# Moving the tiles that TensorE reads to multiples of 256 bytes by padding small tiles, in a two-layer decoder trunk

## The chip, the cores and the metric

One core of a Trainium2 chip. The metric is the device time of one launch, in microseconds. Before the change three runs gave 1027.2, 1028.49 and 1031.6 us; their median, 1028.49 us, is the time before.

## The reference

The kernel computes two decoder layers on x of 512 tokens by 1024. Layer 0 mixes by a gated DeltaNet, layer 1 by a gated short convolution; both have a norm ahead and one behind.

```python
for i in range(DEPTH):                                    # DEPTH = 2
    h = rms_norm(x, pre_norm_w[i])
    y = gated_deltanet_mixer(h, ...) if i == 0 else short_conv_mixer(h, ...)
    x = x + rms_norm(y, post_norm_w[i])

def gated_deltanet_mixer(h, w_in, conv_w, a_log, dt_bias, norm_w, w_out):
    qkv, z, b_logit, a_logit = split(h @ w_in)            # 1024 x 6176
    q, k, v = split(silu(causal_depthwise_conv(qkv, conv_w)))
    q, k = l2_normalize(q), l2_normalize(k)               # 8 heads of 128, each for two of v's 16
    o = chunked_gated_delta_rule(q, k, v, g, beta)        # a triangular solve and a scan over chunks
    return (rms_norm(o, norm_w) * silu(z)) @ w_out        # 2048 x 1024

def short_conv_mixer(h, w_in, conv_w, w_out):
    u, b, c, z = split(h @ w_in)                          # 1024 x 8192
    return (b * causal_depthwise_conv(c * u, conv_w) * silu(z)) @ w_out   # 2048 x 1024
```

All of it is float32.

## The kernel before, in words

**Products.** Each large product is taken in float32r as a sum of three: both operands are split into a high part and a rest, and `mm3` (lines 183 to 186) issues high x high, rest x high and high x rest into one PSUM bank:

```python
nc.tensor.matmul(ps, lhsT=lh, rhs=rh, start=start, stop=False)
nc.tensor.matmul(ps, lhsT=lh, rhs=rl, start=False, stop=False)
nc.tensor.matmul(ps, lhsT=ll, rhs=rh, start=False, stop=stop)
```

`lhsT` is the stationary operand (128 columns of 4 bytes, 512 bytes of a partition), `rhs` the moving one (512 columns, 2048 bytes; 256 columns, 1024 bytes, in a few units of layer 1). Which tiles these are depends on the place:
- `unit` (line 188), the input projections of both layers, into tiles pp: stationary are 128 columns of a weight (tiles whi and wlo, or the two halves of w3), moving are the activations hh and hl (at the very start xh and xl). `weights` (line 171) loads a weight into a raw tile, then ACT or POOL writes the high part and DVE the rest; every third weight goes to w3, so that three are in work.
- `out_products`, the output projection of layer 0, into pa: stationary are the gated outputs of the heads (hh and hl again for heads 0 to 7, oh2 and ol2 for 8 to 11, oh3 and ol3 for 12 to 15), moving are the weights.
- `product`, the output projection of layer 1, into pf: stationary yh and yl, moving whi and wlo (for the last three of 16 steps hh and hl, which then hold weights).

The profile prints names without their numbers: w3 shows as w, oh2 and oh3 as oh, ol2 and ol3 as ol.

**Order.** PE's instructions stand in the order in which the code issues them; chains of smaller work (the norms, the solve, the scan, the gates) are emitted between the steps of products by the class `Pump`, from planned times and a table of corrections. The other engines are ordered by a scheduler. The weights come by the queue of SP.

**Addresses.** Each pool is one stretch of a partition's memory, and its tags follow each other in it: the constants, the weights (wp), the gate values (gt, which ends with par), hh and hl (hp), then es, sm and dl. es holds, after twelve large buffers, two buffers of the tag tm (lines 642 to 646: DVE writes a product to it and subtracts it at once); sm holds small columns, odd among them (line 622, read once by DVE); dl holds ktok, E, zT, nv, S, qg, kT, d2, Vr, then nrm (line 566, written by POOL, read by ACT as a scale) and, behind it, qT, junk and d3. A tile's start is rounded up to 32 bytes and to no more, so a small tile's size sets where all that follow begin. yh, yl and the second w3 lie where dl was.

Of the kernel before, what the change touches and what calls it, by code (L numbers as in the profile page):

```python
# [10 lines left out]
F32 = mybir.dt.float32  # L11
# [7 lines left out]
P = 128  # L19
# [6 lines left out]
NC = T // P  # L26
# [84 lines left out]
def trunk_kernel(ctx, tc, xT, x, cols, rows, eye, post0, pre1, post1, w_in, w_out, sw_in, sw_out, out):  # L111
# [6 lines left out]
    sw_in_v = sw_in.rearrange("(k p) n -> p k n", p=P)  # L118
    sw_out_v = sw_out.rearrange("(k p) n -> p k n", p=P)
    xT_v = xT.rearrange("(k p) t -> p k t", p=P)  # L120

    cst = ctx.enter_context(tc.tile_pool(name="cst", bufs=1))
    dram = ctx.enter_context(tc.tile_pool(name="dram", bufs=1, space=DRAM))
# [37 lines left out]
    def pd(shape, name):  # L161
        return ps_d.tile(shape, F32, tag="pd", name=name)
# [37 lines left out]
    def rsqrt(pool, y, shape, tag, vector=False):  # L200

        r = pool.tile(shape, F32, tag=tag + "r", name=tag + "r")
        t = pool.tile(shape, F32, tag=tag + "t", name=tag + "t")
        nc.vector.tensor_scalar(out=r.bitcast(I32), in0=y.bitcast(I32), scalar1=-0.5, scalar2=float(0x5f3759df),
                                op0=ALU.mult, op1=ALU.add)
        for _ in range(3):
            if vector:
                nc.vector.tensor_tensor(out=t, in0=r, in1=r, op=ALU.mult)
                nc.vector.scalar_tensor_tensor(out=t, in0=t, scalar=-0.5, in1=y, op0=ALU.mult, op1=ALU.mult)
                nc.vector.scalar_tensor_tensor(out=r, in0=t, scalar=1.5, in1=r, op0=ALU.add, op1=ALU.mult)  # L210
            else:
                nc.gpsimd.tensor_tensor(out=t, in0=r, in1=r, op=ALU.mult)
                nc.gpsimd.tensor_tensor(out=t, in0=t, in1=y, op=ALU.mult)
                nc.gpsimd.tensor_scalar(out=t, in0=t, scalar1=-0.5, scalar2=1.5, op0=ALU.mult, op1=ALU.add)
                nc.gpsimd.tensor_tensor(out=r, in0=r, in1=t, op=ALU.mult)
        return r
# [8 lines left out]
    gt = ctx.enter_context(tc.tile_pool(name="gt", bufs=1))  # L225
    hp = ctx.enter_context(tc.tile_pool(name="hp", bufs=1))
    es = ctx.enter_context(tc.tile_pool(name="es", bufs=2))
    sm = ctx.enter_context(tc.tile_pool(name="sm", bufs=2))
# [19 lines left out]
    with ExitStack() as L0:  # L248
        dl = L0.enter_context(tc.tile_pool(name="dl", bufs=2))
# [104 lines left out]
        y, m, t, u, r = (sm.tile([P, NH, NC], F32, tag="gs" + n, name="gs" + n, bufs=1) for n in "ymtur")  # L354
# [140 lines left out]
        def c_kq(gs, kh, w, ps, tl):  # L495
            while not gates_done and kh:
                yield 0.1
            silu = conv_silu(ps, (QK // P if w == 0 else 0) + 2 * gs.g + kh, tl)
            while not gates_done:
                yield 0.1  # L500
            while before_silu:
                before_silu.pop()()
            while gs.g == 0 and (kh or w) and not normed_k:
                yield 0.1
            silu()
            (gs.qT if w else gs.kT)[kh] = tl
            pump.add((c_qnorm if w else c_est)(gs, kh))
            yield 0
# [30 lines left out]
        def norms(tl, ss):  # L539

            junk = dl.tile([P, P], F32, tag="junk", name="junk", bufs=1)
            tok = pd([P, NC, P], "tok")
            for c in range(NC):
                nc.tensor.transpose(out=tok[:, c], in_=tl[:, c * P:(c + 1) * P], identity=ident)
            pump.pe(0.43, False)
            for c in range(NC):
                last_sq = nc.scalar.activation(junk, tok[:, c], AF.Square, accum_out=ss[:, c:c + 1])
            nc.vector.tensor_scalar_add(ss, ss, EPS)
            return tok, last_sq
# [10 lines left out]
        def c_est(gs, kh):  # L560
            g = gs.g
            while not gates_done or (g > 1 and not groups[g - 2].done):
                yield 1
            kT = gs.kT[kh]
            if kh == 0:
                gs.nrm = dl.tile([P, 2, NC], F32, tag="nrm", name="nrm")
                gs.epsa = dl.tile([P, 2, NC], F32, tag="epsa", name="epsa")
                gs.bp, gs.bpe = (dl.tile([P, 4, NC], F32, tag=n, name=n) for n in ("bp", "bpe"))
                gs.E = dl.tile([P, 16, P], F32, tag="E", name="E", bufs=2)
            yield (11 if g else 4,)  # L570
            ss = sm.tile([P, NC], F32, tag="ssn", name="ssn")
            tok, last_sq = norms(kT, ss)
            ktok = dl.tile([P, NC, P], F32, tag="ktok", name="ktok", bufs=4)
            kte = 0 if g == 0 else 1
            if kte == 1:
                nc.scalar.copy(ktok, tok)
            gs.ktok[kh] = ktok
            normed_k.append(1)
            kk = pd([P, NC, P], "kk")
            for c in range(NC):  # L580
                s = slice(c * P, (c + 1) * P)
                nc.tensor.matmul(kk[:, c], lhsT=kT[:, s], rhs=kT[:, s], start=True, stop=True)
            pump.pe(0.9, False)
            rk2 = sm.tile([P, 1, NC], F32, tag="rk2", name="rk2")
            nc.vector.reciprocal(rk2[:, 0], ss)
            h2, g2 = slice(2 * kh, 2 * kh + 2), slice(4 * g + 2 * kh, 4 * g + 2 * kh + 2)
            nc.vector.tensor_tensor(out=gs.bp[:, h2], in0=beta[:, g2], in1=rk2.to_broadcast([P, 2, NC]), op=ALU.mult)
            for r in range(2):
                hl_, h = 2 * kh + r, 4 * g + 2 * kh + r
                if g == 0:  # L590
                    dt = dt0[h]
                else:
                    dt = es.tile([P, NC, P], F32, tag="dt", name="dt")
                    nc.sync.dma_start(out=dt, in_=dt_d[h])
                for c in range(NC):
                    nc.scalar.activation(dt[:, c], dt[:, c], AF.Copy, scale=gs.bp[:, hl_, c:c + 1])
                last_e = nc.vector.tensor_tensor(out=gs.E[:, 4 * hl_:4 * hl_ + 4], in0=kk, in1=dt, op=ALU.mult)
                nc.sync.dma_start(out=dt_d[h], in_=dt)
            if kte == 0:
                nc.vector.tensor_copy(ktok, tok)  # L600
            if g == 0:
                fence[:] = last_e, last_sq
            nc.vector.tensor_tensor(out=gs.bpe[:, h2], in0=gs.bp[:, h2], in1=edec[:, g2], op=ALU.mult)
            rk = rsqrt(sm, ss, [P, NC], "rk")
            nc.gpsimd.tensor_tensor(out=gs.nrm[:, kh], in0=ss, in1=rk, op=ALU.mult)  # L605
            gs.est += 1
            if gs.est == 2:
                pump.add(c_solve(gs))

        def c_solve(gs):  # L610
# [7 lines left out]
            E = gs.E  # L618
            blk = lambda i, n=32: slice(n * i, n * i + n)
            if not parity:  # L620
                odd = sm.tile([P, 1], F32, tag="odd", name="odd", bufs=1)
                nc.vector.tensor_reduce(out=odd, in_=ident.rearrange("p (a c k) -> p c a k", c=2, k=16)[:, 1],
                                        op=ALU.add, axis=mybir.AxisListType.XY)
                par = gt.tile([P, 16, 2], F32, name="par")
                nc.vector.tensor_copy(par[:, :, 1:2], odd[:, :, None].to_broadcast([P, 16, 1]))
                nc.vector.tensor_scalar(out=par[:, :, 0:1], in0=par[:, :, 1:2], scalar1=-1.0, scalar2=1.0,
                                        op0=ALU.mult, op1=ALU.add)
                parity.append(par)
# [10 lines left out]
            for i in range(31, 0, -1):  # L639
                m0 = i // 2  # L640
                w = 16 - m0
                t = es.tile([P, 136], F32, tag="tm", name="tm")
                tv = t[:, :i * w].rearrange("p (m j) -> p m j", j=i)
                nc.vector.tensor_tensor(out=tv, in0=N[:, i:i + 1, 0:i].to_broadcast([P, w, i]),
                                        in1=X[:, m0:, i:i + 1].to_broadcast([P, w, i]), op=ALU.mult)
                nc.vector.tensor_tensor(out=X[:, m0:, 0:i], in0=X[:, m0:, 0:i], in1=tv, op=ALU.subtract)  # L646
# [541 lines left out]
```

## Time and profile before

| | us |
|---|---|
| median of three runs | 1028.49 (1027.2 to 1031.6) |
| the profiled execution | 1028.76 |
| its span, first to last instruction | 1026.6 |
| PE busy | 974.4 (95%) |
| DVE busy | 612.3 (60%) |
| ACT busy | 420.6 (41%) |
| POOL busy | 235.4 (23%) |
| mean granted clock of TensorE | 0.978 of 2.4 GHz |

The layers follow each other in time: layer 0 takes until about 570 us, the input projections of layer 1 until about 930 us, and the last product with the last norm the rest. A product's duration in the trace covers its way through the array, so neighbours overlap: what a product costs in a row of products is the distance between two starts. The addresses of operands aren't in the trace; they come from the program that was built.

### The profile page before, as it was taken

Reading aid. Unit: us, or ns where it says so; the run is one execution under the profiler, and the core shown is the slowest. Engines: PE = TensorE matmul, PEld = TensorE weight load, DVE = VectorE, ACT = ScalarE, POOL = GpSimd, SP = SyncE. Lnnn points to the kernel's source line nnn. Section 1 sums busy time; section 2 is a strip of 40 time slices with the busy share of each in tenths; the row PEclk is TensorE's granted clock in tenths of the full one; section 3 lists DMA queues with packets and bytes.
Section 4 is the critical chain, followed back from the end, with each engine's and each line's share of the span. In section 5 each row is a group of like instructions: output and inputs, shape, how many; then the busy total and the mean of one; then the engine's idle time right before and its main releaser. Section 6 shows DMA issues by size and latency. Waiting matters only on the chain.

```text
span 1026.6 us, 14732 instructions
## 1 busy us (share of the span) xinstructions
PE 974.4 (95%) x5430; PEld 805.7 (78%) x5430; DVE 612.3 (60%) x1100; ACT 420.6 (41%) x1002; POOL 235.4 (23%) x446
## 2 busy tenths in 40 slices
PE   7957999989999999999998999999999999999997
PEld 5845778877788788888776899888888888888885
DVE  8678998746986784734469976433433433333133
ACT  4575764526545553334212554232222322322123
POOL 6264631344135223335633000000000000000001
PEclk9987999999999999999999999999999999999999
DMA  6334673255235622793645556333233332323322
GB/s 193 89 109 124 211 240 84 63 156 162 76 100 151 178 63 82 218 330 128 197 145 182 163 169 188 110 91 103 83 101 93 92 103 84 102 82 102 103 83 82
DMA packets 172391, 133.91 MB, mean 130 GB/s; under 512 B 6272, under 2 KB 146176, under 8 KB 171936
## 3 DMA queue, kind: packets, MB, share of 16 engines
q1 hardware_dynamic: 172176, 132.88, 43.1%
q8 instruction: 43, 0.70, 0.3%
q14 instruction: 28, 0.23, 0.1%
q10 hardware_dynamic: 144, 0.09, 0.0%
HBM read 117.16 MB, written 15.79 MB: 130 GB/s over the span
## 4 chain that ended last, share of the span: by engine, by line
PE 75%; DVE 9%; DMA 6%; ACT 4%; issue 3%; POOL 2%; SPq 0%; POOLq 0%; DVEq 0%; ACTq 0%
PE pp L184 17%; PE pp L186 17%; PE pp L185 17%; PE pf L185 3%; PE pf L184 2%; PE pf L186 2%; PE pa L186 2%; PE pa L185 2%; PE pa L184 2%; PE u L758 2%; DVE wlo L167 1%; DMA gb<-gt_d 1%; PE po L792 1%; PE psn L772 1%; PE p L748 1%
## 5 line engine op out<-in xcount | busy, mean ns | idle before, releaser
L184 PE MATMUL pp<-hh,whi 128*128 128x512 f32 (+1 forms) x624 | 239.2, 383 | 5.1 <-DVE acc L470 2.1
L185 PE MATMUL pp<-hl,whi 128*128 128x512 f32 (+1 forms) x624 | 233.3, 374 | 1.0 <-DVE r L987 1.0
L186 PE MATMUL pp<-hh,wlo 128*128 128x512 f32 (+1 forms) x624 | 233.3, 374 | 0.0
L167 DVE TENSOR_TENSOR wlo<-wraw,whi 128x1024 fp32r<-128x1024 f32 x115 | 141.4, 1229 | 135.5 <-ACT whi L166 110.1
L166 ACT CAST whi<-wraw 128x1024 fp32r<-128x1024 f32 x64 | 67.2, 1050 | 189.8 <-PE pp L185 112.2
L184 PEld LDWEIGHTS pp<-hh,whi 128*128 128x128 f32 x624 | 119.1, 191 | 26.8 <-POOL nrm L605 2.5
L186 PEld LDWEIGHTS pp<-hh,wlo 128*128 128x128 f32 x624 | 118.8, 190 | 22.2
L185 PEld LDWEIGHTS pp<-hl,whi 128*128 128x128 f32 x624 | 119.1, 191 | 21.1 <-DVE hl L167 1.2
L184 PE MATMUL pp<-hh,w 128*128 128x512 f32 (+1 forms) x304 | 116.1, 382 | 0.0
L186 PE MATMUL pp<-hh,w 128*128 128x512 f32 (+1 forms) x304 | 113.2, 373 | 1.1 <-DVE w L167 1.1
L185 PE MATMUL pp<-hl,w 128*128 128x512 f32 (+1 forms) x304 | 113.2, 372 | 0.0
L1144 POOL TENSOR_TENSOR ob<-ob,ytNa 128x384 f32<-128x384 f32 x2 | 2.1, 1040 | 458.0 <-ACT ob L1143 458.0
L166 POOL CAST whi<-wraw 128x1024 fp32r<-128x1024 f32 x51 | 62.1, 1219 | 94.0 <-PE pp L185 60.8
L167 DVE TENSOR_TENSOR w<-wraw,w 128x1024 fp32r<-128x1024 f32 x50 | 62.6, 1252 | 33.8 <-ACT w L166 31.7
L186 PEld LDWEIGHTS pp<-hh,w 128*128 128x128 f32 x304 | 57.3, 189 | 12.4 <-DVE w L167 1.5
L184 PEld LDWEIGHTS pp<-hh,w 128*128 128x128 f32 x304 | 57.5, 189 | 10.3 <-issue 0.4
L185 PEld LDWEIGHTS pp<-hl,w 128*128 128x128 f32 x304 | 57.3, 189 | 9.7
L470 DVE SCALAR_TENSOR_TENSOR acc<-pp,col,acc 128x511 f32<-128x511 f32 (+2 forms) x72 | 53.6, 745 | 14.4 <-ACT acc L467 13.5
L166 ACT CAST w<-wraw 128x1024 fp32r<-128x1024 f32 x25 | 26.2, 1047 | 67.8 <-PE pp L185 48.6
L185 PE MATMUL pf<-wlo,yh 128*128 128x512 f32 x104 | 41.5, 399 | 0.0
L184 PE MATMUL pf<-whi,yh 128*128 128x512 f32 x104 | 41.0, 394 | 0.0
L646 DVE TENSOR_TENSOR Na<-Na,tm 128x126 f32<-128x126 f32 (+22 forms) x124 | 39.4, 317 | 2.7
(310 smaller groups left out, 1724.8 us busy)
## 6 DMA issues: line engine op xcount, KB each, us to landing
wraw<-in_sw_in_dram SPq DMA_DIRECT2D x76, 512.0 KB, 4.0
wraw<-in_w_in_dram SPq DMA_DIRECT2D x47, 512.0 KB, 4.0
wraw<-in_w_out_dram SPq DMA_DIRECT2D x32, 512.0 KB, 4.1
wraw<-in_sw_out_dram SPq DMA_DIRECT2D x16, 512.0 KB, 3.5
eg<-gt_d SPq DMA_DIRECT2D x16, 256.0 KB, 4.2
dtq<-dt_d SPq DMA_DIRECT2D x16, 256.0 KB, 3.9
gb<-gt_d SPq DMA_DIRECT2D x3, 1024.0 KB, 6.6
dt_d<-gb SPq DMA_DIRECT2D x3, 1024.0 KB, 4.9
```

Of the source, the lines that this page charges most:

```text
L166: (nc.scalar.copy if hi_eng is None else hi_eng.tensor_copy)(dst_hi, src)
L167: nc.vector.tensor_tensor(out=dst_lo, in0=src, in1=dst_hi.bitcast(F32), op=ALU.subtract)
L184: nc.tensor.matmul(ps, lhsT=lh, rhs=rh, start=start, stop=False)
L185: nc.tensor.matmul(ps, lhsT=lh, rhs=rl, start=False, stop=False)
L186: nc.tensor.matmul(ps, lhsT=ll, rhs=rh, start=False, stop=stop)
L470: nc.vector.scalar_tensor_tensor(out=acc[:, s:], in0=ps[:, :T - s], scalar=w(j), in1=acc[:, s:], op0=ALU.mult, op1=ALU.add)
L646: nc.vector.tensor_tensor(out=X[:, m0:, 0:i], in0=X[:, m0:, 0:i], in1=tv, op=ALU.subtract)
L748: nc.tensor.matmul(p1[:, 2 * kh:2 * kh + 2], lhsT=gs.kT[kh][:, s], rhs=S[:, 2 * kh:2 * kh + 2], start=True, stop=True)
L758: nc.tensor.matmul(u[:, a], lhsT=gs.E[:, 4 * a + c], rhs=X[:, a] if c else gs.nv[a][:, c], start=True, stop=True)
L772: nc.tensor.matmul(psn[:, 2 * kh:2 * kh + 2], lhsT=gs.ktok[kh][:, c], rhs=Vk[:, 2 * kh:2 * kh + 2], start=True, stop=True)
L792: nc.tensor.matmul(po[:, a], lhsT=gs.qkd[a][:, c], rhs=Vr[:, a], start=c == 0, stop=True)
L1144: nc.gpsimd.tensor_tensor(out=ob[:, m], in0=ob[:, m], in1=yt[c][:, m], op=ALU.add)
```

## The change

Four small tiles are allocated larger than what is used of them: par twice as large (128 bytes more), tm 768 bytes for 544, odd 64 for 4, nrm 96 for 32. The names then stand for the part that was there before. (An empty line at the top of the function moves all later line numbers by one.)

```diff
--- before.py
+++ after.py
@@ -118,6 +118,7 @@
     sw_in_v = sw_in.rearrange("(k p) n -> p k n", p=P)
     sw_out_v = sw_out.rearrange("(k p) n -> p k n", p=P)
     xT_v = xT.rearrange("(k p) t -> p k t", p=P)
+
 
     cst = ctx.enter_context(tc.tile_pool(name="cst", bufs=1))
     dram = ctx.enter_context(tc.tile_pool(name="dram", bufs=1, space=DRAM))
@@ -563,7 +564,7 @@
                 yield 1
             kT = gs.kT[kh]
             if kh == 0:
-                gs.nrm = dl.tile([P, 2, NC], F32, tag="nrm", name="nrm")
+                gs.nrm = dl.tile([P, 6, NC], F32, tag="nrm", name="nrm")[:, :2]
                 gs.epsa = dl.tile([P, 2, NC], F32, tag="epsa", name="epsa")
                 gs.bp, gs.bpe = (dl.tile([P, 4, NC], F32, tag=n, name=n) for n in ("bp", "bpe"))
                 gs.E = dl.tile([P, 16, P], F32, tag="E", name="E", bufs=2)
@@ -618,10 +619,10 @@
             E = gs.E
             blk = lambda i, n=32: slice(n * i, n * i + n)
             if not parity:
-                odd = sm.tile([P, 1], F32, tag="odd", name="odd", bufs=1)
+                odd = sm.tile([P, 16], F32, tag="odd", name="odd", bufs=1)[:, 0:1]
                 nc.vector.tensor_reduce(out=odd, in_=ident.rearrange("p (a c k) -> p c a k", c=2, k=16)[:, 1],
                                         op=ALU.add, axis=mybir.AxisListType.XY)
-                par = gt.tile([P, 16, 2], F32, name="par")
+                par = gt.tile([P, 2, 16, 2], F32, name="par")[:, 0]
                 nc.vector.tensor_copy(par[:, :, 1:2], odd[:, :, None].to_broadcast([P, 16, 1]))
                 nc.vector.tensor_scalar(out=par[:, :, 0:1], in0=par[:, :, 1:2], scalar1=-1.0, scalar2=1.0,
                                         op0=ALU.mult, op1=ALU.add)
@@ -639,7 +640,7 @@
             for i in range(31, 0, -1):
                 m0 = i // 2
                 w = 16 - m0
-                t = es.tile([P, 136], F32, tag="tm", name="tm")
+                t = es.tile([P, 192], F32, tag="tm", name="tm")
                 tv = t[:, :i * w].rearrange("p (m j) -> p m j", j=i)
                 nc.vector.tensor_tensor(out=tv, in0=N[:, i:i + 1, 0:i].to_broadcast([P, w, i]),
                                         in1=X[:, m0:, i:i + 1].to_broadcast([P, w, i]), op=ALU.mult)
```

No engine's list of instructions differs, in operations, shapes, order or waits. What differs is where tiles lie. The offset of a tile's start from the last multiple of 256 bytes:

| tiles | before | after |
|---|---|---|
| whi, wlo, the raw weights | 0 | 0 |
| hh, hl | 128 | 0 |
| acc, vT, dt, qkd (es, ahead of tm) | 128 | 0 |
| tm, its two buffers | 128, 160 | 0, 0 |
| X, eg (es, behind tm) | 192 | 0 |
| ktok, E and oh3, zT and ol3, w3, nv, S, qg, kT and oh2, d2, Vr | 160 | 0 |
| yh, yl (layer 1) | 160 | 0 |
| qT and ol2, junk, d3 (behind nrm) | 32 | 0 |
| ident, ones, utri, ltri (constants) | 128 | 128 |
| g of the gates, rx | 64, 224 | 128, 32 |
| ac and zs, ob (layer 1, for DVE, ACT and DMA alone) | 0, 192 | 96, 32 |

By pairs of operands (moving/stationary), the products of `mm3` are, before: 1518 at 128/0, 120 at 0/128 and 2 at 128/128; 796 at 128/160, 420 at 0/160, 24 at 0/32, 150 at 160/0, 82 at 160/128, 72 at 160/160 and 8 at 160/32; those of 256 columns 384 at 128/0 and 192 at 128/160. After: 3180 at 0/0, 12 at 0/128, and 576 of 256 columns at 0/0.

## Rows read from the trace of the kernel before

**Rows 1.** The page: busy time by engine, and PE and DVE by slices.

```profile
PE 974.4 (95%) x5430; PEld 805.7 (78%) x5430; DVE 612.3 (60%) x1100; ACT 420.6 (41%) x1002; POOL 235.4 (23%) x446
...
PE   7957999989999999999998999999999999999997
...
DVE  8678998746986784734469976433433433333133
```

**Rows 2.** The page: chain that ended last, by engine and by line.

```profile
PE 75%; DVE 9%; DMA 6%; ACT 4%; issue 3%; POOL 2%; SPq 0%; POOLq 0%; DVEq 0%; ACTq 0%
PE pp L184 17%; PE pp L186 17%; PE pp L185 17%; PE pf L185 3%; PE pf L184 2%; PE pf L186 2%; PE pa L186 2%; PE pa L185 2%; PE pa L184 2%; PE u L758 2%; DVE wlo L167 1%; DMA gb<-gt_d 1%; PE po L792 1%; PE psn L772 1%; PE p L748 1%
```

**Rows 3.** Busy time of the engines by stretch (columns in its second line).

```profile
core 0: us, PE busy (x) PEld busy (x) DVE busy (x) ACT busy (x) POOL busy (x), PEclk, DMA share, GB/s
0.00:100.00 100.00, 75.01 (x348) 58.67 (x349) 75.83 (x135) 58.71 (x132) 47.55 (x62) 0.88 0.42 127
...
200.00:300.00 100.00, 93.72 (x643) 78.91 (x642) 70.33 (x161) 49.89 (x167) 38.00 (x94) 0.97 0.42 121
...
600.00:700.00 100.00, 100.00 (x599) 88.49 (x598) 51.23 (x65) 37.66 (x56) 0.00 (x0) 1.00 0.46 133
...
900.00:1000.00 100.00, 100.00 (x431) 80.60 (x430) 29.93 (x30) 23.21 (x25) 0.00 (x0) 1.00 0.32 95
...
544.70:547.30 2.60, 2.60 (x8) 1.99 (x7) 2.53 (x6) 0.86 (x4) 2.60 (x1) 0.51 0.85 269
```

**Rows 4.** Timeline of PE, hh against whi: start, duration, instruction.

```profile
852.85 0.40 PE L184 MATMUL pp<-hh,whi 128*128 128x512 f32 x1
853.09 0.40 PE L185 MATMUL pp<-hl,whi 128*128 128x512 f32 x1
...
862.61 0.40 PE L184 MATMUL pp<-hh,whi 128*128 128x512 f32 x1
```

**Rows 5.** Timeline of PE, hh against w3 (printed w).

```profile
847.02 0.40 PE L186 MATMUL pp<-hh,w 128*128 128x512 f32 x1
...
851.92 0.39 PE L186 MATMUL pp<-hh,w 128*128 128x512 f32 x1
```

**Rows 6.** Timeline of PE, the last product.

```profile
949.22 0.39 PE L184 MATMUL pf<-whi,yh 128*128 128x512 f32 x1
949.45 0.40 PE L185 MATMUL pf<-wlo,yh 128*128 128x512 f32 x1
949.69 0.39 PE L186 MATMUL pf<-whi,yl 128*128 128x512 f32 x1
...
956.22 0.39 PE L184 MATMUL pf<-whi,yh 128*128 128x512 f32 x1
```

**Rows 7.** Timeline of PE at half clock.

```profile
544.74 0.62 PE L184 MATMUL pa<-whi,oh 128*128 128x512 f32 x1
...
547.29 0.63 PE L184 MATMUL pa<-w,oh 128*128 128x512 f32 x1
```

**Rows 8.** Timeline of PE, w3 against oh3 and ol3, behind that stretch.

```profile
548.84 0.39 PE L186 MATMUL pa<-w,ol 128*128 128x512 f32 x1
549.07 0.39 PE L184 MATMUL pa<-w,oh 128*128 128x512 f32 x1
...
550.20 0.39 PE L186 MATMUL pa<-w,ol 128*128 128x512 f32 x1
```

**Rows 9.** Timeline of PE, w3 against oh3 and ol3, two other places.

```profile
515.31 0.40 PE L184 MATMUL pa<-w,oh 128*128 128x512 f32 x1
...
516.71 0.49 PE L184 MATMUL pa<-w,oh 128*128 128x512 f32 x1
...
557.91 0.40 PE L184 MATMUL pa<-w,oh 128*128 128x512 f32 x1
...
560.71 0.40 PE L184 MATMUL pa<-whi,oh 128*128 128x512 f32 x1
```

**Rows 10.** Timeline of PE, products of 256 columns.

```profile
581.32 0.28 PE L184 MATMUL pp<-hh,w 128*128 128x256 f32 x1
...
583.80 0.28 PE L184 MATMUL pp<-hh,w 128*128 128x256 f32 x1
...
584.87 0.28 PE L184 MATMUL pp<-hh,whi 128*128 128x256 f32 x1
...
589.73 0.28 PE L186 MATMUL pp<-hh,wlo 128*128 128x256 f32 x1
```

**Rows 11.** Chain in order of time: start, us, what.

```profile
129.01 5.80 DMA dt_d<-gb
...
332.92 7.48 DMA og_d<-ohs
```

**Rows 12.** DMA issues: size each, median us to landing.

```profile
dt_d<-dt SPq DMA_DIRECT2D x12, 256.0 KB, 3.3
og_d<-ohs SPq DMA_DIRECT2D x12, 256.0 KB, 2.6
...
dt_d<-gb SPq DMA_DIRECT2D x4, 256.0 KB, 2.1
```

## The prediction

> **What bounds the kernel now.** I read the page first. PE is busy 95% of the span, and in the 40 slices its digit is 9 from about 100 us to the end almost without a break, while DVE has 60% and ACT 41% [rows 1]. The chain that ended last says the same in another way: 75% of it is PE, and the nine PE entries for the destinations pp, pf and pa at lines 184 to 186 add up to 64% (17+17+17, 3+2+2, 2+2+2) [rows 2]. These are the products of `mm3`, so 0.64 x 1026.6 = 657 us of the path consist of one kind of instruction. The table by stage shows no other engine near PE from 600 us on (PE 100 of 100 us, DVE 51 to 30) [rows 3]. DMA has 6% of the chain [rows 2].
>
> Then I read the timeline for the distance from the start of one product to the next. The busy figure of one product (0.39 to 0.40 us) says nothing on the rate, since products overlap. With 512 columns at 2.4 GHz the columns alone are 512/2.4 = 213.3 ns. The trace has more: 42 products from 852.85 to 862.61 us, 232.4 ns each [rows 4]; 21 from 847.02 to 851.92 us, 233.3 ns [rows 5]; 30 from 949.22 to 956.22 us, 233.3 ns [rows 6]. At the granted clock of 0.5 six products take 2.55 us, 425 ns each, which is 512/1.2 = 427 and nothing more [rows 3, 7]. So at the upper level some 19 ns of 233 are not columns, and at the lower level they are absent. These 19 ns, 657 x 19/233 = 54 us of the path, are all that addresses could win in the products.
>
> **The change part by part.** No instruction is added, removed or moved: each engine has the same list in the same order with the same waits. Four tiles get larger, and by that every tile allocated behind them starts elsewhere. Of `mm3`'s 3768 products, 3192 have 512 columns and 576 have 256. Before, no pair has both operands at a multiple of 256 bytes; after, all but 12 of the 3768 have (the address table stands with the change). The four padded tiles themselves are used by DVE and POOL in the same shapes, so nothing is charged for them.
>
> Addresses of each sort can be compared inside this one trace, as the buffers differ:
> - moving operand at 128 (hh, hl), stationary at 0 (whi, wlo): 232.4 ns [rows 4]
> - moving at 128, stationary at 160 (the third buffer w3, printed as w): 233.3 ns [rows 5]
> - moving at 0 (whi, wlo), stationary at 160 (yh, yl): 233.3 ns [rows 6]
> - both at 160 (w3 with the last four heads, oh3 and ol3): six products from 548.84 to 550.20 us, 226.7 ns each [rows 8]; with operands of the same offsets six from 515.31 to 516.71 us, 233.3 ns, and twelve from 557.91 to 560.71 us, 233.3 ns [rows 9].
> So putting one operand at a multiple of 256 buys at most 0.9 ns (0.4%), whichever operand it is. What both at 0 do is not in the trace. Two rows are near to it. By the distance from a boundary it is the pair 128/0, for 0 and 128 are the two offsets that are multiples of 128: 232.4 ns. By equal offset of the two operands it is the pair 160/160: (6 x 226.7 + 18 x 233.3)/24 = 231.7.
>
> The path now: 1640 of the 3192 wide products have their operands at 0 and 128 (232.4), 1552 have one at 160 or 32 (233.3), mean 232.8. On the path 657 us / 232.8 ns = 2820 wide products, so 1 ns is worth 2.8 us. With the first near row the change gives 232.8 - 232.4 = 0.4 ns, or 1.1 us; with the second 1.1 ns, or 3.1 us. I take the second, since equal offsets are what the change makes of every pair: 3.1 us. The 256-column products bear on this little: from 584.87 to 589.73 us 41 of them take 118.5 ns each at 128/0, and from 581.32 to 583.80 us 21 take 118.1 ns at 128/160 [rows 10], so there the worse offset is even faster by 0.4 ns; 576 x 0.4 = 0.2 us, left out.
>
> The bounds: the best a product can get is 213.3 ns, 19.5 less than now, 55 us; the best run seen, 226.7, gives 6.1 x 2.8 = 17 us. The other way, the slowest spacing that comes regularly is 238 ns, the step behind L185 in the last product (949.45 to 949.69 us is 0.24) [rows 6]; if every product had it the cost would be 5.2 x 2.8 = 15 us.
>
> Other engines and DMA: DVE, ACT and POOL are off the path in the long stages, and whichever of their tiles move start at a multiple of 32 bytes before and after. The Trainium skill, SBUF — State Buffer, section Specifications (TRN2), gives lines of 16 bytes for reads of SBUF; a multiple of 32 starts such a line before and after, so by that rule the whole change is worth nothing and the time stays at 1028.8; the spread from 226.7 to 233.3 at one pair of addresses shows that start addresses are at least not the only thing that sets the spacing.
>
> DMAs out of tiles that move: dt_d<-gb 5.80 us and og_d<-ohs 7.48 us are the longest of them on the chain [rows 11]; the trace has none of this size from a 256-byte offset to compare, so I bound them by nothing and by the whole difference between the stores of 256 KB, 2.1 us (dt_d<-gb) to 3.3 us (dt_d<-dt) [rows 12], 1.2 us each and 2.4 for both, either way, and take nothing. The Trainium skill, DMA: Bandwidth & Descriptors, section How a descriptor splits into AXI transactions, says that a transfer that doesn't start on 256 bytes fetches from the boundary below; a 2048-byte row would then fetch 9 blocks where 8 do, and 13.3 us on the chain would lose an estimated ninth, 1.5 us. No run here shows it yet.
>
> Sum against the profiled execution: 1028.76 us with a span of 1026.6, 2.2 us around it; 1028.76 - 3.1 = 1025.7. The median of the three timed runs, 1028.49, lies 0.3 below the profiled one; I keep 1025.7.
>
> **The rivals.**
> 1. Both operands on a boundary lock every product at the short spacing of 226.7 ns: 17 us, 1012. For it: six in a row at 226 to 227 ns, and the only stretch with equal offsets has it. Against: 18 products with the same offsets at 233.3, and the 226.7 begins right behind a stretch of half clock, which may have set its phase.
> 2. The 19 ns come from crossing boundaries and vanish: 216 ns, 16.8 x 2.8 = 47 us, 982. Against: a stationary operand at 0 and a moving operand at 0, each with another partner, leave 232.4 and 233.3. The Trainium skill, TensorE: Matmul & The Clock Gate, section Back-to-back issue gap, has N/2.4 + 2.5 ns, 216 for 512 columns; the trace disagrees in every run of wide products at 2.4 GHz that I looked at, so this page is what speaks for it.
> 3. Slower: both operands now start on the same place of a 256-byte block in every product, and the two reads meet each time. Place: all of `mm3`. Price: up to the 238 ns spacing, 15 us, 1043; it decides from 1.8 ns on (5.1 / 2.8), a mean spacing over 234.6. For it: an offset that is off by 32 beats one at a boundary in the 256-column products. Against: the stretches with equal offsets at 160 are not above 233.3.
> 4. The claim holds for `mm3` only: ident, ones, utri and ltri stay at 128, and the transposes and small products that read them can't gain. This leaves the sum as it is; nothing of it was counted.
> A shift of a microsecond or two in when PE waits can also add or remove one of the short stretches at half clock (the mean clock is 0.88 in the first 100 us and 0.97 from 200 to 300 [rows 3]); it is noise of 2 us to the forecast.
>
> **How the numbers follow.** A difference under 0.5% (5.1 us) can't be told from no change in this kernel. Chances: forecast (spacing 231 to 234.5, from 5 us faster to 5 us slower) 0.50; rival 1 and spacings between 227 and 231 0.32; rival 2 0.06; rival 3 0.12. So faster 0.38, same 0.50, slower 0.12. The likeliest case alone is 1022 to 1032. The range for 8 in 10 reaches down to rival 1, less 2 us of noise, 1010, and up to 1034, where a part of rival 3 is still inside; outside stay rival 2 and the worse half of rival 3.
>
> **What will show it.** In the profile after, the spacing of the wide products at full clock is the whole test: for hh/whi (232.4 before), for hh/w3 and for pf (233.3 before). About 231.7 in all three bears the forecast out; 226.7 is rival 1, 216 rival 2, over 234.6 rival 3. The order of the chain's entries should stay as it is. The prediction is wrong if the spacing stays at 232 to 233 and the time moves by more than 5 us: then a wait or a transfer did it, which this sum has at nothing.

## The result, and the profile after

The change made the kernel faster: 1016.27 us, median of 6 runs (1014.69 to 1019.41), against 1027.92 us for the kernel before beside it (6 runs, 1026.97 to 1031.60). The ratio is 0.988, interval 0.986 to 0.991. That is 11.7 us, more than the 5.1 us that can be told from no change. The profiled execution took 1017.51 us with a span of 1015.6, which is 11.0 us below the span before.

From the page of the kernel after (lines 185 to 187 are the three products of `mm3`, one line further down than before), busy time by engine and the chain that ended last, to lay beside [rows 1, 2]:

```profile
PE 960.8 (95%) x5430; PEld 805.5 (79%) x5430; DVE 611.7 (60%) x1100; ACT 420.1 (41%) x1002; POOL 239.6 (24%) x446
...
PE 70%; DVE 13%; DMA 7%; ACT 4%; issue 3%; POOL 3%; SPq 0%; POOLq 0%; DVEq 0%; ACTq 0%
PE pp L185 16%; PE pp L187 16%; PE pp L186 16%; PE pf L185 2%; PE pf L187 2%; PE pf L186 2%; DVE tm L645 2%; DVE wlo L168 2%; DMA eg<-gt_d 2%; DVE Na L647 2%; PE pa L186 1%; PE pa L187 1%; DMA gb<-gt_d 1%; PE pa L185 1%; PE u L759 1%
```

The counts of instructions are the same as before on every engine, and so are the busy times of DVE and ACT to within 0.6 us. Only PE is shorter, by 13.6 us; POOL has 4.2 us more, which the kernel all_128 below, with the same spacing of products, doesn't have (235.6 us). On the chain PE falls from 75% to 70%, and DVE rises from 9% to 13%: the solve (tm, line 645, and Na, line 647) is now among the fifteen dearest entries, where it was not. That this follows from the shorter products isn't shown: all_128 has 74% PE and 10% DVE and neither entry, so the chain of one execution can go either way there.

The table by stage of the kernel after (first line: columns), for [rows 3]:

```profile
core 0: us, PE busy (x) PEld busy (x) DVE busy (x) ACT busy (x) POOL busy (x), PEclk, DMA share, GB/s
0.00:100.00 100.00, 74.03 (x337) 58.57 (x338) 72.83 (x126) 57.16 (x128) 46.66 (x61) 0.85 0.41 127
...
900.00:1000.00 100.00, 100.00 (x443) 82.81 (x442) 29.52 (x32) 25.75 (x32) 0.00 (x0) 1.00 0.27 85
```

From 900 to 1000 us PE is busy throughout, at a granted clock of 1.00 in both kernels, and does 443 products where it did 431. The first 100 us go the other way: 337 instructions in place of 348, at a clock of 0.85 in place of 0.88.

The test that the prediction named is the spacing. The timeline of PE in the kernel after (start, duration, instruction), hh against whi, for [rows 4]:

```profile
846.39 0.39 PE L185 MATMUL pp<-hh,whi 128*128 128x512 f32 x1
846.62 0.39 PE L186 MATMUL pp<-hl,whi 128*128 128x512 f32 x1
...
855.91 0.39 PE L185 MATMUL pp<-hh,whi 128*128 128x512 f32 x1
```

These are 42 products in 9.52 us: 226.7 ns, where 232.4 stood. The same view, hh against w3 for [rows 5] and the last product for [rows 6]:

```profile
840.27 0.39 PE L185 MATMUL pp<-hh,w 128*128 128x512 f32 x1
...
845.03 0.39 PE L185 MATMUL pp<-hh,w 128*128 128x512 f32 x1
...
934.11 0.39 PE L185 MATMUL pf<-whi,yh 128*128 128x512 f32 x1
...
940.91 0.39 PE L185 MATMUL pf<-whi,yh 128*128 128x512 f32 x1
```

21 products in 4.76 us and 30 in 6.80 us, 226.7 ns both, where 233.3 stood. All three sorts have the spacing that the prediction gave to rival 1. The products of 256 columns, for [rows 10], went the other way:

```profile
582.50 0.28 PE L185 MATMUL pp<-hh,whi 128*128 128x256 f32 x1
...
586.47 0.28 PE L185 MATMUL pp<-hh,whi 128*128 128x256 f32 x1
```

33 products in 3.97 us, 120.3 ns, where 118.5 and 118.1 stood.

### The profile page after: what moved, and what is told of

It is laid out like the page before. It is cut to its first block, busy times and chain, and to the rows that moved or that the text cites. A ratio compares the mean times of both kernels' runs of the same rounds, so it can differ in the third digit from the quotient of the medians.

```text
span 1015.6 us, 14732 instructions
## 1 busy us (share of the span) xinstructions
PE 960.8 (95%) x5430; PEld 805.5 (79%) x5430; DVE 611.7 (60%) x1100; ACT 420.1 (41%) x1002; POOL 239.6 (24%) x446
## 4 chain that ended last, share of the span: by engine, by line
PE 70%; DVE 13%; DMA 7%; ACT 4%; issue 3%; POOL 3%; SPq 0%; POOLq 0%; DVEq 0%; ACTq 0%
PE pp L185 16%; PE pp L187 16%; PE pp L186 16%; PE pf L185 2%; PE pf L187 2%; PE pf L186 2%; DVE tm L645 2%; DVE wlo L168 2%; DMA eg<-gt_d 2%; DVE Na L647 2%; PE pa L186 1%; PE pa L187 1%; DMA gb<-gt_d 1%; PE pa L185 1%; PE u L759 1%
## 5 line engine op out<-in xcount | busy, mean ns | idle before, releaser
L185 PE MATMUL pp<-hh,whi 128*128 128x512 f32 (+1 forms) x624 | 236.7, 379 | 4.5 <-DVE acc L471 2.2
L185 PE MATMUL pp<-hh,w 128*128 128x512 f32 (+1 forms) x304 | 114.9, 378 | 0.7 <-DVE acc L471 0.7
L187 PE MATMUL pp<-hh,w 128*128 128x512 f32 (+1 forms) x304 | 112.0, 368 | 1.3 <-DVE w L168 1.3
L167 POOL CAST whi<-wraw 128x1024 fp32r<-128x1024 f32 x51 | 65.4, 1283 | 84.7 <-PE pp L186 58.0
L645 DVE TENSOR_TENSOR tm<-Na 128x126 f32<-128x126 f32 (+22 forms) x124 | 38.9, 314 | 2.9
```

The lines of the kernel that those rows point to most:

```text
L167: (nc.scalar.copy if hi_eng is None else hi_eng.tensor_copy)(dst_hi, src)
```

## Where the 11.0 us of span came from

PE runs the same list of products in both kernels, so each product can be matched with itself, and the distance to the next one compared. The sums over three stretches of the trace before, "wide" being pairs of 512-column products that follow each other directly in both traces:

```
stretch (before)   wide pairs   ns before -> after   sum      everything else
0 to 566 us        1265         232.6 -> 228.7       -4.9 us  +2.0 us
566 to 640 us         1                               0       +2.0 us
640 us to the end  1630         232.8 -> 226.7      -10.0 us   0
```

From 640 us on nothing but the spacing differs, and 1630 x 6.1 ns is the gain there. Up to 566 us the same products give only 3.9 ns each. The reason is in the timeline of the kernel after, behind a stretch of other work:

```profile
222.28 0.39 PE L186 MATMUL pp<-hl,w 128*128 128x512 f32 x1
222.50 0.39 PE L187 MATMUL pp<-hh,w 128*128 128x512 f32 x1
222.73 0.40 PE L185 MATMUL pp<-hh,w 128*128 128x512 f32 x1
222.97 0.39 PE L186 MATMUL pp<-hl,w 128*128 128x512 f32 x1
223.20 0.40 PE L187 MATMUL pp<-hh,w 128*128 128x512 f32 x1
223.43 0.39 PE L185 MATMUL pp<-hh,w 128*128 128x512 f32 x1
223.66 0.39 PE L186 MATMUL pp<-hl,w 128*128 128x512 f32 x1
223.89 0.39 PE L187 MATMUL pp<-hh,w 128*128 128x512 f32 x1
224.11 0.39 PE L185 MATMUL pp<-hh,w 128*128 128x512 f32 x1
```

The steps are 224, 231, 236, 228, 233, 231, 226 and 227 ns (the trace has nanoseconds), and they stay at 226 and 227. The row of products began at 221.26 us: here it takes ten products after an interruption until the spacing is 226.7, and until then it is 231 on the mean, the first step left out. This is called settling below, and a row that has come to its steady spacing is called locked. Over all rows of wide products up to 566 us, the first nine steps after an interruption have 230.4 ns in the mean and the later ones 226.9; in the kernel before they have 232.4 and 232.8. Up to 566 us the rows of products are short and often interrupted; from 640 us on there is no interruption, and the spacing is locked throughout.

The rest, +4.0 us, stands in this one profiled execution outside the wide products: 0.9 us of it is the 256-column products (576 x 1.5 ns, from the mean over all of them), the first 100 us have +3.1 at the lower clock, 100 to 277 us has -2.4. The kernel all_128 below, with the same spacing, has +1.0 us in all for the same sum. The spans of the six executions of the changed kernel go from 1012.4 to 1017.1 us. So most of the 4.0 us is of the size by which one execution differs from the next, and isn't shown to be a property of the change.

## The experiments

**offsets.** A program that does nothing but series of 36 products, in threes as `mm3` issues them; moving and stationary operand start at chosen byte offsets (modulo 256) of their partitions. Its main lines, with ... for what stands between them (S lists the columns of the moving operand, its offset, the stationary operand's offset and columns, and the type):

```diff
+PER = 36
...
+    for n, m, s, w, kind in S:
...
+        for i in range(PER):
...
+            nc.tensor.matmul(ps[:w, :n], lhsT=st[:, a:a + w], rhs=mt[:, b:b + n], start=i == 0, stop=i == PER - 1)
```

> Leaves out the whole decoder: it only streams products, 34 series of 36, with operands at chosen offsets (moving/stationary, in bytes from a multiple of 256), the two stationary tiles and two moving tiles taken in turn as mm3 takes them; its time means nothing, the spacing of starts in each series does. Theory 'equal offsets' (the spacing depends on the difference of the two offsets modulo 256): 512 columns at 0/0, 16/16, 32/32, 64/64, 160/160 and 0/256 settle at 226.7 ns, all others at 232 to 234. Rival 'boundary' (both must start at a multiple of 256): only 0/0 and 0/256 settle at 226.7, equal pairs elsewhere at 232 to 234. Rival 'history' (the lock depends on what ran before, not on addresses): no order by offsets. Stationary operand of 32 columns: 226.7 or less whatever the offset if the two reads disturb each other, unchanged at 232 to 233 if the moving read is slow alone. bf16 (half the bytes): 216 at every offset if the reads of SBUF are what costs. 256 columns: 120.0 at 0/0 and 118 to 119 elsewhere, as the two traces have it.

Measured, the settled spacing of the last 18 products of a series in ns, offsets as moving/stationary:

```
512 columns, equal:    0/0 226.7  0/256 226.7  32/32 226.7  64/64 226.7  160/160 226.7  16/16 233.3  4/4 237.8
512, stationary off:   0/16 226.7  0/32 233.3  0/64 233.3  0/96 234.4  0/128 232.5  0/160 233.3  0/192 228.9  0/224 233.2  0/384 232.0
512, moving off:       32/0 233.4  64/0 228.9  128/0 232.7  192/0 233.3  4/0 237.2
256 columns:           0/0 120.3  32/32 120.0  0/32 118.4  0/64 117.8  0/96 117.2  0/128 118.6  0/192 117.8
32 stationary columns: 0/0 231.6  0/32 240.0  0/160 233.1
bf16, 512 columns:     0/0 215.8  0/32 215.8  0/128 215.8
```

The timeline of this program for 0/64, 0/256, 64/64, 4/4 and the 256 columns of 0/0 and 0/96, each row part of one series (start, time from the first start to the last end, number of products):

```profile
35.68 7.40 PE L81 MATMUL ps<-mov,sta 128*128 128x512 f32 x31
...
87.69 5.38 PE L81 MATMUL ps<-mov,sta 128*128 128x512 f32 x23
...
153.57 6.06 PE L81 MATMUL ps<-mov,sta 128*128 128x512 f32 x26
...
168.61 7.77 PE L81 MATMUL ps<-mov,sta 128*128 128x512 f32 x32
...
185.83 3.53 PE L81 MATMUL ps<-mov,sta 128*128 128x256 f32 x28
...
197.81 4.15 PE L81 MATMUL ps<-mov,sta 128*128 128x256 f32 x34
```

Less the last product's own 0.39 or 0.40 us (0.28 with 256 columns) and divided by one less than the count, they give 233.3, 226.8, 226.8, 237.7, 120.4 and 117.3 ns. So for 512 columns it is the two offsets against each other, modulo 256, that go with the spacing, and 0 is worth no more than 64 or 160. 0/192 and 64/0, the same difference modulo 256, agree (228.9), and so do 0/64 and 192/0 (233.3). The 256-column products are at their worst where the wide ones are at their best. The stationary operand of 32 columns was to show whether fewer columns of it take less; it is no faster than 128 columns at any of the three offsets (233.1 against 233.3 at 0/160 is the nearest), and why is open. bf16 has 215.8 ns at all three pairs, as the expectation had it for the case that the reads of SBUF are what costs; since bf16 differs from fp32r in more than its bytes, this doesn't show the cause. Two values, 0/16 at 226.7 and 16/16 at 233.3, fit no rule of equal offsets: each stood right behind a series at just that spacing. PE doesn't rest between the series of this program, so the pairs that no later run takes up (4/4, 4/0, 256 columns, 32 stationary columns) stand on one series each.

**offsets2.** So twelve pairs were run forwards and then backwards, 48 products each, with a rest of PE between series. The line that makes the rest, against the program offsets:

```diff
-    pp = ctx.enter_context(tc.tile_pool(name="pp", bufs=4, space=PSUM))
+    pp = ctx.enter_context(tc.tile_pool(name="pp", bufs=1, space=PSUM))
```

> Leaves out the decoder again: 24 series of 48 wide products, twelve pairs of offsets forward and then backward, and PE waits for the copy of the result between series, so that each starts from rest; nothing else runs beside it. It is to separate address from history, which the first run of this sort leaves open for 16/16 (233.3 behind a series at 233.3) and 0/16 (226.7 behind one at 226.7), and to show 64/0 against 0/64. Address alone: each pair has the same settled spacing in both passes, 226.7 for equal offsets (8/8 and 16/16 too), 228.9 for 64/0 and 0/192, 233.3 for 0/64 and 192/0. History: 16/16, 0/16 or others differ between the passes. In the decoder's layer 0 the wide products have 228.7 ns in the mean and not 226.7. If that is the start behind every interruption, the first ten products of the 0/0 series take about 231 ns here too, with no other engine at work; if it is the traffic of other engines, they take 226.7 from the first on.

```
            0/0    64/64  96/96  64/0   0/192  0/128  0/16   0/32   0/64   192/0  16/16  8/8
forwards    226.7  226.7  226.7  228.9  228.9  231.9  233.3  233.3  233.3  233.3  230.0  231.4
backwards   226.7  226.7  226.7  228.9  228.9  231.9  233.3  233.3  233.3  233.3  231.1  231.9
```

The timeline of this program, 64/64 on the way forwards and 0/64 on the way back:

```profile
96.82 8.32 PE L77 MATMUL ps<-mov,sta 128*128 128x512 f32 x36
...
254.71 8.10 PE L77 MATMUL ps<-mov,sta 128*128 128x512 f32 x34
```

(8.32 - 0.39)/35 = 226.6 and (8.10 - 0.40)/33 = 233.3 ns. Ten of the twelve pairs settle at the same value both ways, whatever went before; 16/16 and 8/8 differ by 1.1 and 0.5 ns. 0/16 at 226.7 was the state of the series ahead of it, carried on where PE did not rest. The expectation had 8/8 and 16/16 at 226.7 with the other equal pairs, and that missed: of the equal offsets tried, the multiples of 32 bytes lock at 226.7, and 4, 8 and 16 don't. The slow start is here as well, with no other engine at work: behind the first step of 337 ns, 0/0 backwards has 224, 231, 236, 228, 233, 231 ns and then 226, 227, 227, the very steps of the kernel from 222.28 us on; 64/64 forwards is at 226.7 from its second step, and backwards has 231.5 on the mean of the eight steps behind its first.

**no_par, par_only, all_128.** Three kernels that give each sort of product its own pair of offsets. no_par is the change without the padding of par, so that hh, w3 and yh are at 128 and whi at 0; par_only is the kernel before with that padding alone, so that hh is at 0 beside whi, and w3 and yh at 32; all_128 is the whole change with 128 bytes more behind the constants, so that every operand of `mm3` is at 128 and none at a multiple of 256.

```diff
 no_par
-                par = gt.tile([P, 2, 16, 2], F32, name="par")[:, 0]
+                par = gt.tile([P, 16, 2], F32, name="par")
 par_only (against the kernel before)
-                par = gt.tile([P, 16, 2], F32, name="par")
+                par = gt.tile([P, 2, 16, 2], F32, name="par")[:, 0]
 all_128
-    rowp = cst.tile([P, 32], F32, name="rowp")
+    rowp = cst.tile([P, 64], F32, name="rowp")[:, :32]
```

> The change without its padding of par: hh, hl, w3, yh, yl and the rest lie at 128, whi and wlo at 0. Products of hh with w3 are then 128/128, those with whi 128/0, the last product 0/128. Equal offsets: hh/w3 settle at 226.7 ns, hh/whi and pf stay at 232.4; of layer 1's wide products 416 gain 6.6 ns, 2.7 us, and pf 0.3 us: about 1025 us. Boundary: all stay at 232 to 233, about 1027.5 us.

> The padding of par alone: hh and hl at 0 like whi and wlo; w3, yh and yl at 32. Both theories: hh/whi settle at 226.7 ns, hh/w3 (0/32) and pf (0/32) stay at 233; 832 wide products of layer 1 gain 5.7 ns, 4.7 us, less 0.6 us for 384 of 256 columns, layer 0 gives one or two more: about 1022 us. History: as the full change or as before, by chance.

> The change with 128 bytes of padding at the end of the constants, so that everything from the raw weights on lies 128 bytes later: all pairs of mm3 at 128/128, nothing at 256. Equal offsets: as the change, 226.7 ns and about 1016 us. Boundary: 232 to 233 ns and about 1027 us.

The timeline of no_par, hh against w3 (128/128) and then hh against whi (128/0):

```profile
845.85 0.39 PE L185 MATMUL pp<-hh,w 128*128 128x512 f32 x1
...
849.93 0.39 PE L185 MATMUL pp<-hh,w 128*128 128x512 f32 x1
...
850.62 0.40 PE L185 MATMUL pp<-hh,whi 128*128 128x512 f32 x1
...
860.38 0.40 PE L185 MATMUL pp<-hh,whi 128*128 128x512 f32 x1
```

18 products in 4.08 us, 226.7 ns, and directly behind them 42 in 9.76 us, 232.4 ns. The timeline of par_only, hh against whi (0/0) and the last product (0/32):

```profile
848.14 0.39 PE L184 MATMUL pp<-hh,whi 128*128 128x512 f32 x1
...
857.66 0.39 PE L184 MATMUL pp<-hh,whi 128*128 128x512 f32 x1
...
936.89 0.40 PE L184 MATMUL pf<-whi,yh 128*128 128x512 f32 x1
...
943.89 0.40 PE L184 MATMUL pf<-whi,yh 128*128 128x512 f32 x1
```

42 in 9.52 us, 226.7, and 30 in 7.00 us, 233.3 ns. The timeline of all_128, hh against whi at 128/128:

```profile
843.36 0.39 PE L185 MATMUL pp<-hh,whi 128*128 128x512 f32 x1
...
852.88 0.39 PE L185 MATMUL pp<-hh,whi 128*128 128x512 f32 x1
```

42 in 9.52 us again. The times, against the same runs of the kernel before (1028.10 us, 19 runs), with the gain of the matched wide products from 640 us on:

```
           median (runs)    ratio [interval]         wide products from 640 us on
no_par     1026.19 (10)     0.9973 [0.9951, 0.9994]   -3.2 us
par_only   1022.35 (10)     0.9944 [0.9925, 0.9963]   -4.6 us
all_128    1015.46 (4)      0.9886 [0.9848, 0.9924]  -10.0 us
```

In each kernel exactly the sort with equal offsets is at 226.7 and the others stay between 232 and 234. all_128 gains what the change gains (0.9886 against 0.9883) with no operand of `mm3` at a multiple of 256. So the change works by making the two offsets equal; that they are 0 has no part in it. Nothing is left over for the transposes and small products either: from one to the next of the same kind they take as long in the kernel after and in all_128 as before (by the line numbers of the kernel before, 76 products of line 792 took 111.5 ns before and 111.4 in both, and 45 transposes by ident on line 525 took 108.8 before, 108.6 and 108.7), and the whole gain from 640 us on is in the wide products.

**mm_0213.** The order of the work was planned with a price of 0.217 us for a wide product. This kernel is the change, planned anew with a lower one:

```diff
-MM = 0.217
+MM = 0.213
```

> The change with the planner's cost of a wide product set from 0.217 to 0.213 us, the ratio by which the products of layer 0 became faster (228.7/232.7), so that the small chains are emitted at other places of PE's order. If the change's gain in layer 0 is partly lost because the plan no longer fits the rate, some 1 to 2 us come back: 1014 to 1015 us. If the corrections of the table fit the old places alone, it loses: 1018 to 1025 us. The spacing of products in layer 1 stays at 226.7 ns either way.

1037.95 us (5 runs, 1034.79 to 1040.06) against 1029.37 (8 runs) for the kernel before: ratio 1.0091, interval 1.0058 to 1.0124, so 2.1% more than the change has (1.0091/0.9883). The expectation of a time missed: it had 1014 to 1015 or 1018 to 1025 us. The page of mm_0213:

```profile
PE 961.8 (93%) x5430; PEld 806.3 (78%) x5430; DVE 613.8 (59%) x1100; ACT 424.6 (41%) x1004; POOL 227.5 (22%) x446
```

The table by stage up to the first product of 256 columns, where layer 1 begins, first of mm_0213 and then of the change:

```profile
0.00:581.90 581.90, 518.99 (x3206) 427.86 (x3206) 411.70 (x822) 277.62 (x794) 223.37 (x442) 0.96 0.47 146
```

```profile
0.00:564.10 564.10, 516.79 (x3206) 425.75 (x3206) 409.73 (x822) 273.37 (x792) 235.49 (x442) 0.97 0.49 150
```

PE is busy as long as in the change over the whole span (961.8 and 960.8 us), and layer 1's wide products stay at 226.7 ns as expected; but PE stands idle for 1033.2 - 961.8 = 71 us of the span, where the change has 55. All of the loss lies ahead of layer 1: with the same 3206 products that part takes 17.8 us longer, and PE is idle in it for 63 us in place of 47. Which of the moved small chains makes PE wait is not shown. So a plan whose corrections were fitted to one price lost more by a new price than the truer price could bring.

## Why the prediction was right, and where it failed

**What held.** The bound was named rightly: the wide products of `mm3` set the time, the addresses bear on the spacing of products and on nothing else that the runs show, no instruction moved, and from 640 us on the whole difference is the spacing. The direction held, but the forecast of 3.1 us lay below the 5.1 us that it could tell from no change. That the time lies in the range is owed to the range's width: 1016.27 us is outside the likeliest case (1022 to 1032) and inside only because the range reaches down to rival 1, and the sign that was to bear the forecast out, 231.7 ns in all three sorts, did not come. That the lower clock hides the effect, which [rows 7] showed, holds too: in the first series of offsets the products at 1.2 GHz are 427 ns apart with equal offsets.

**The step that failed** is the size taken for equal offsets: "I take the second, since equal offsets are what the change makes of every pair: 3.1 us". The near row was the right one of the two, and its value was wrong. 231.7 was the mean of six products at 226.7 [rows 8] and eighteen at 233.3 [rows 9], and these were taken for a spread at one pair of addresses. They are two states in order of time: not yet locked, and locked. Between the rows shown in [rows 9] the trace of the kernel before has:

```profile
559.10 0.39 PE L186 MATMUL pa<-w,ol 128*128 128x512 f32 x1
559.32 0.39 PE L184 MATMUL pa<-w,oh 128*128 128x512 f32 x1
559.55 0.40 PE L185 MATMUL pa<-w,oh 128*128 128x512 f32 x1
559.79 0.39 PE L186 MATMUL pa<-w,ol 128*128 128x512 f32 x1
560.02 0.40 PE L184 MATMUL pa<-w,oh 128*128 128x512 f32 x1
560.25 0.39 PE L185 MATMUL pa<-w,oh 128*128 128x512 f32 x1
560.48 0.39 PE L186 MATMUL pa<-w,ol 128*128 128x512 f32 x1
```

The steps are 224, 231, 235, 229, 232 and 231 ns: those of the kernel after from 222.28 us on, to within a nanosecond. The next, to 560.71 us, is 227, and there the series with equal offsets ends. No such series in the kernel before ran for more than twelve products, and settling took eleven steps in this one and ten at 222 us in the kernel after, so the mean of [rows 9] measured the settling. Read in order, the rows said that 226.7 is where such a series goes, and the forecast would have been rival 1.

**Rival 1** was the mechanism: 226.7 ns in `mm3`'s wide products. Its doubt, that the 226.7 of [rows 8] had been set by the half clock ahead of it, fell with offsets and offsets2, where equal offsets lock without one. Its price of 17 us was too high: 1 ns was taken to be worth 2.8 us over the whole path, while up to 566 us the slow start leaves 3.9 of the 6.1 ns, so that the wide products gave 10.0 + 4.9 = 14.9 us; and 11 to 13 us of that reached the end (11.7 with the change, 12.6 with all_128). The count of 2820 wide products on the path was too high as well: the 657 us hold the 576 products of 256 columns, which got no faster, at 576 x 118.5 ns = 68 us. And up to 566 us less than half of the chain is wide products. The chain of the kernel before in that stretch:

```profile
by line: PE pp L184 10.4%; PE pp L186 9.9%; PE pp L185 9.8%; issue 4.0%; PE pa L186 3.1%; PE pa L185 3.0%; PE pa L184 3.0%; PE u L758 2.7%; DMA gb<-gt_d 2.3%; PE po L792 2.2%; DVE wlo L167 2.1%; PE psn L772 1.8%; PE p L748 1.7%; DVE Na L646
```

The six entries pp and pa add up to 39.2% of 566 us, 222 us, or some 950 of the 1265 wide products, so that some 2580 are on the path in all. An estimate from these rows is 950 x 3.9 ns = 3.7 us up to 566 us, 10.0 us from 640 us on, less 0.9 us for the 256 columns: 12.8 us, near to what came.

**Rival 2** (216 ns) fell: no fp32r series of 512 columns with any offsets is below 226.7. The gap of 216 ns for 512 columns in the Trainium skill, TensorE: Matmul & The Clock Gate, section Back-to-back issue gap, is met by bf16 (215.8 at three pairs of offsets), and not by the fp32r products of this kernel.

**Rival 3** (equal offsets make the two reads meet) was wrong for 512 columns and right in sign for 256: 120.0 to 120.3 ns with equal offsets, 117.2 to 118.6 with others. The 0.2 us that the prediction left out there is 0.9 us, a loss.

**Rival 4** (the claim holds for `mm3` alone) was true (the small products of all_128's paragraph take as long as before), and changed nothing in the sum, as it said.

**No effect at all**, which followed from the lines of 16 bytes in the Trainium skill, SBUF — State Buffer, section Specifications (TRN2), is refuted for TensorE's operands: all offsets from 0 to 224 in steps of 32 start such a line, and the spacing goes from 226.7 to 234.4 among them. The measurement decides.

**The DMAs** were taken at nothing. On the chain of the kernel after (start, us, what), for [rows 11]:

```profile
131.32 5.67 DMA dt_d<-gb
...
331.29 7.26 DMA og_d<-ohs
```

They are 0.13 and 0.22 us shorter, 0.35 in all. But the second piece, at 7.26 us here, has 7.29 us in par_only, 7.37 in no_par and 7.49 in all_128, where its tile lies on no multiple of 256, and 5.58 in mm_0213, where it lies as in the change. The estimate of 1.5 us, worked out from the Trainium skill, DMA: Bandwidth & Descriptors, section How a descriptor splits into AXI transactions, is not reached; the 0.35 us are within what kernels with other or the same addresses differ by, and no run here takes these transfers by themselves, so an effect of the address is not shown.

**What stays open.** Why the spacing has just these levels, why equal offsets of 4, 8 and 16 bytes don't lock where multiples of 32 do, and what differs between a series that starts locked and one that settles first. The share of the gain lost up to 640 us is read from matched traces and one chain, and was not tried by a kernel of its own. Giving the 256-column products unequal offsets again would bring an estimated 576 x 3.1 ns = 1.8 us (120.3 at 0/0 less 117.2 at 0/96), less than can be told here, and was not tried.

## What to carry to other kernels

Where TensorE runs fp32r products of 512 columns back to back at 2.4 GHz, let the moving and the stationary operand start at the same byte offset modulo 256, at a multiple of 32; which of the multiples it is made no difference here, and 2.6% of their time was in it. Look at the starts of consecutive products in the trace rather than at the busy figure, and read a short series step by step: a mean over fewer than a dozen products behind an interruption is the mean of its settling. A plan whose corrections were fitted to one price need not gain by a truer one: here a price 2% truer cost 2.1%.

## What the runs showed of the hardware that was not expected

- The spacing of wide fp32r products goes with the difference of the two operands' offsets modulo 256: 226.7 ns at none, 228.9 where the moving operand is 64 bytes ahead, about 232 at 128, 233 to 234.4 at the other multiples of 32, and 237 to 238 where one or both are at 4 bytes. The pairs tried are equal ones, those with one operand at 0, and 128/160 in the kernel before.
- For 256 columns the order is reversed (120.0 to 120.3 at none, 117.2 at 0/96), and for bf16 there is none at the three pairs tried (215.8).
- Equal offsets at 8 and 16 bytes do not lock (230 to 232).
- The lock needed ten or eleven steps after an interruption in the kernels and six to nine in offsets2, in much the same sequence of steps, and was there at once in two series of offsets2 (64/64 and 96/96 forwards); and a series can carry the spacing of the one ahead of it (0/16 at 226.7 behind 0/0, 233.3 behind a rest).
- A stationary operand of 32 columns in place of 128 made the products no faster: 231.6 at 0/0 where 128 columns have 226.7.
